# The first stage of a decoder trunk: weights loaded early into the room of later blocks, the conditioning row from TensorE, and each block's k-tiles ahead of its value parts

## The chip, the cores and the metric

One core of a Trainium2 chip runs the whole program. The metric is the device time of one execution in microseconds, the median of several runs. Before the change three runs took 2672.34, 2677.94 and 2679.41 us; the median is 2677.94.

## The reference, cut to what matters

The program is a two-layer decoder trunk for 256 positions of width 2048 in float32: a layer of RWKV-7 time mixing, a layer of latent attention, each followed by a squared-ReLU MLP. Ahead of every mixer stands a norm whose scale and shift come from a conditioning vector `c`:

```python
c_act = jax.nn.silu(c)
mod = (c_act @ ada_w[l] + ada_b[l]).reshape(B, N_MOD, 1, D)
h = rms_norm(x, norm_g[l, 0]) * (1.0 + scale_m) + shift_m
...
xx = token_shift(h) - h
xs = h[None] + xx[None] * mu[:, None, None, :]        # r, k, v, w, a, g
rkv = jnp.einsum('jbtd,jde->jbte', xs[:3], w_rkv)
w_log = -jax.nn.softplus(-(w0 + jnp.tanh(xw @ w1) @ w2)) - 0.5
a = jax.nn.sigmoid(a0 + (xa @ a1) @ a2)
g = jax.nn.sigmoid(xg @ g1) @ g2
```

The change touches the first stage alone: scale and shift of layer 0, the six shifted mixtures `xs`, the value projection, and the low-rank products behind `w`, `a` and `g`.

## The kernel before, in words

Products are made in split precision: a number is the sum of a high part, rounded to `fp32r`, and a low part, and a product is three matmuls (high x high, high x low, low x high). `hilo` (line 161) makes the parts: ACT casts, and another engine, DVE unless told otherwise, subtracts (line 163). Every weight comes through `load` (line 165): a tile `raw` of 128x2048, 1 MB, from the pool `wp`, which has three of them, and a DMA on SP's queue. That queue is in order: a load whose `raw` is still in use holds all behind it.

The first stage goes over the 16 k-tiles (128 input features each) in four blocks `cb` of four. For a block it needs

- scale and shift of its 512 features: `ada_pe` (line 271) for modulations 1 and 0, four loads `ada` each. PE multiplies them by the activated condition (line 278, `adap`), ACT copies, four matmuls sum (line 267, `modc`), DVE adds the bias (line 269, `mod`);
- small low-rank weights `lwa` and `lg1`, split once for the block;
- for each k-tile two transposes of the normed input (line 448, `trx`), `h` on ACT, the difference `d` to the position before, and six mixtures `xs` on DVE (line 457), each split by `hilo`. Mixtures 3, 4, 5 go into 12 low-rank matmuls `lr`, mixture 2 is kept for the block (`xsv`), mixtures 0 and 1 (r and k) are kept for the second stage in the four tiles `xsr`, `xsk` (high and low) of all 16 k-tiles.

`value_part(cb, n)` multiplies a block's `xsv` by one load `wv`: 24 matmuls `pv` (lines 202 to 204), whose result ACT copies or DVE adds to `V` (line 425). In the code the four value parts of block `cb - 1` stand ahead of the k-tiles of block `cb`, each with the next two steps of `ada_pe`:

```python
for n in range(4):
    next(at, 0)
    next(at, 0)
    if cb:
        value_part(cb - 1, n)
```

After block 3 its own value parts follow, and then the conditioning row `crow`, `silu(c)` repeated on 128 partitions: it is loaded as 1 MB, and ACT and DVE form exponential, sum, reciprocal and product in four pieces (lines 500 to 503). The remaining modulations are made from it on DVE during later stages (line 300, `ada_steps`). The second stage begins with `project_rk` (line 530): loads `wr` and `wk`, splits, and matmuls `rk`.

A scheduler turns this into one order for each engine; an engine runs its instructions strictly in that order. The pools set the waits: `p3` keeps three buffers of each k-tile tile (`h`, `d`, `xs`, `xlh`, `xll`), `split` two of each half weight.

## Time and profile before

| | |
|---|---|
| median of three runs | 2677.94 us |
| the profiled execution | 2670.03 us |
| its span | 2668.3 us |
| PE, DVE, ACT, POOL busy | 95%, 72%, 50%, 4% of the span |
| first stage | until about 221 us |
| DMA | 595.85 MB, 223 GB/s over the span |

The span is what the profiler saw of the engines in one execution; the execution's own time is 1.7 us longer. A row of a timeline gives the start from the span's beginning, how long it took, and, in brackets, how long the engine had been idle and which instruction ended that. A matmul's row includes its latency, so that rows of PE overlap.

### The profile page before, as it was taken

Reading aid. Unit: us, or ns where it says so; the run is one execution under the profiler, and the core shown is the slowest. Engines: PE = TensorE matmul, PEld = TensorE weight load, DVE = VectorE, ACT = ScalarE, POOL = GpSimd, SP = SyncE. Lnnn points to the kernel's source line nnn. Section 1 sums busy time; section 2 is a strip of 40 time slices with the busy share of each in tenths; the row PEclk is TensorE's granted clock in tenths of the full one; section 3 lists DMA queues with packets and bytes.
Section 4 is the critical chain, followed back from the end, with each engine's and each line's share of the span. In section 5 each row is a group of like instructions: output and inputs, shape, how many; then the busy total and the mean of one; then the engine's idle time right before and its main releaser. Section 6 shows DMA issues by size and latency. Waiting matters only on the chain.

```text
span 2668.3 us, 43143 instructions
## 1 busy us (share of the span) xinstructions
PE 2544.7 (95%) x16936; PEld 2191.4 (82%) x16936; DVE 1924.1 (72%) x3691; ACT 1327.1 (50%) x2361; POOL 105.2 (4%) x174
## 2 busy tenths in 40 slices
PE   6896899999998999999999998999899999999998
PEld 2576788888876899889988987788798998999896
DVE  4787788788877588888888757877667555555555
ACT  3543566666654544444444545554554444444443
POOL 0000111111100100000000002000010000000000
PEclk7998999999999999999999998999999999999999
DMA  8863444444456488888888831656657555555553
GB/s 314 302 235 144 171 167 155 158 167 159 148 207 269 172 333 329 332 334 324 339 321 329 327 141 72 237 188 241 233 183 270 185 187 191 186 188 189 189 190 127
DMA packets 88045, 595.85 MB, mean 223 GB/s; under 512 B 10144, under 2 KB 14496, under 8 KB 16800
## 3 DMA queue, kind: packets, MB, share of 16 engines
q1 hardware_dynamic: 87840, 593.08, 60.4%
q8 instruction: 133, 2.18, 0.3%
q14 instruction: 72, 0.59, 0.1%
HBM read 590.94 MB, written 2.10 MB: 222 GB/s over the span
## 4 chain that ended last, share of the span: by engine, by line
PE 87%; DVE 6%; ACT 3%; DMA 2%; issue 1%; POOL 1%; SPq 0%; DVEq 0%; ACTq 0%; POOLq 0%
PE pup L209 9%; PE pup L208 9%; PE pup L207 9%; PE pd L202 9%; PE pd L203 9%; PE pd L204 9%; PE rk L207 2%; PE rk L209 2%; PE rk L208 2%; PE pm L622 2%; DVE wlo L163 1%; PE po L203 1%; PE po L204 1%; PE po L202 1%; PE pv L203 1%
## 5 line engine op out<-in xcount | busy, mean ns | idle before, releaser
L163 DVE TENSOR_TENSOR wlo<-raw,whi 128x1024 fp32r<-128x1024 f32 (+1 forms) x737 | 877.3, 1193 | 478.2 <-ACT whi L162 475.4
L162 ACT CAST whi<-raw 128x1024 fp32r<-128x1024 f32 (+1 forms) x737 | 751.1, 1022 | 893.5 <-PE pd L204 380.6
L209 PE MATMUL pup<-hh,wlo 128*128 128x256 f32 x1920 | 543.5, 283 | 0.0
L207 PE MATMUL pup<-hh,whi 128*128 128x256 f32 x1920 | 543.4, 283 | 0.0
L208 PE MATMUL pup<-hl,whi 128*128 128x256 f32 x1920 | 543.3, 283 | 0.0
L202 PE MATMUL pd<-whi,uh 128*128 128x512 f32 x1024 | 398.7, 389 | 0.0
L203 PE MATMUL pd<-wlo,uh 128*128 128x512 f32 x1024 | 398.5, 389 | 0.0
L204 PE MATMUL pd<-whi,ul 128*128 128x512 f32 x1024 | 398.4, 389 | 0.0
L300 DVE SCALAR_TENSOR_TENSOR raw<-raw,crow 128x1024 f32<-128x1024 f32 x320 | 389.1, 1226 | 9.1 <-DMA raw<-in_adat_dram 9.0
L207 PEld LDWEIGHTS pup<-hh,whi 128*128 128x128 f32 x1920 | 368.6, 192 | 0.5
L208 PEld LDWEIGHTS pup<-hl,whi 128*128 128x128 f32 x1920 | 368.5, 192 | 0.5
L209 PEld LDWEIGHTS pup<-hh,wlo 128*128 128x128 f32 x1920 | 368.6, 192 | 0.0
L204 PEld LDWEIGHTS pd<-whi,ul 128*128 128x128 f32 x1024 | 192.2, 188 | 40.0
L202 PEld LDWEIGHTS pd<-whi,uh 128*128 128x128 f32 x1024 | 192.3, 188 | 39.5
L203 PEld LDWEIGHTS pd<-wlo,uh 128*128 128x128 f32 x1024 | 192.3, 188 | 39.3
L209 PE MATMUL rk<-xsrh,wlo 128*128 128x256 f32 x256 | 76.6, 299 | 15.7 <-DVE wlo L163 15.7
L207 PE MATMUL rk<-xskh,whi 128*128 128x256 f32 x256 | 81.2, 317 | 1.9 <-ACT whi L162 1.4
L207 PE MATMUL rk<-xsrh,whi 128*128 128x256 f32 x256 | 76.9, 301 | 3.0 <-ACT whi L162 3.0
L209 PE MATMUL rk<-xskh,wlo 128*128 128x256 f32 x256 | 75.1, 294 | 0.8 <-DVE wlo L163 0.8
L208 PE MATMUL rk<-xskl,whi 128*128 128x256 f32 x256 | 74.6, 291 | 0.0
L208 PE MATMUL rk<-xsrl,whi 128*128 128x256 f32 x256 | 74.5, 291 | 0.0
L209 PEld LDWEIGHTS rk<-xsrh,wlo 128*128 128x128 f32 x256 | 51.4, 201 | 16.8 <-DVE wlo L163 16.1
(433 smaller groups left out, 4094.1 us busy)
## 6 DMA issues: line engine op xcount, KB each, us to landing
raw<-in_adat_dram SPq DMA_DIRECT2D x160, 1024.0 KB, 6.8
raw<-in_up_dram SPq DMA_DIRECT2D x128, 1024.0 KB, 4.8
raw<-in_dn_dram SPq DMA_DIRECT2D x128, 1024.0 KB, 4.8
raw<-in_ada_dram SPq DMA_DIRECT2D x32, 1024.0 KB, 6.3
raw<-in_wv_dram SPq DMA_DIRECT2D x16, 1024.0 KB, 5.5
raw<-in_wr_dram SPq DMA_DIRECT2D x16, 1024.0 KB, 4.7
raw<-in_wk_dram SPq DMA_DIRECT2D x16, 1024.0 KB, 4.9
raw<-in_wo_dram SPq DMA_DIRECT2D x16, 1024.0 KB, 5.2
```

What stands on the lines that cost most here:

```text
L162: ACT.copy(hi, x)
L163: return eng.tensor_sub(lo, x, hi.bitcast(F32))
L202: PE.matmul(ps, lh, rh, start=start, stop=False)
L203: PE.matmul(ps, lh, rl, start=False, stop=False)
L204: PE.matmul(ps, ll, rh, start=False, stop=stop)
L207: PE.matmul(ps, wh, xh, start=start, stop=False)
L208: PE.matmul(ps, wh, xl, start=False, stop=False)
L209: PE.matmul(ps, wl, xh, start=False, stop=stop)
L300: DVE.scalar_tensor_tensor(raw[:, s], raw[:, s], 1.0, crow[:, s], ALU.mult, ALU.mult, accum_out=part[:, kt, half : half + 1])
L622: PE.matmul(pm[h][:, c * T : (c + 1) * T], lhs[hp, c * P : (c + 1) * P], AR[hp, c, :, :].rearrange("p x t -> p (x t)"), start=True, stop=True)
```

## The change

**Rooms.** The r and k mixtures lie no longer in four tiles of 16 k-tiles, but in one tile `xs{b}` per block b of 128x4x4x256, 16 KB per partition. Until block b writes its mixtures, its tile's room takes two weights of 1 MB: `load` asks `spot`, and after three loads into `raw` come two into each room that is still ahead (six before and in block 0 as the counter runs, then four, then two, none in block 3).

**Conditioning row.** `crow` is a tile for the whole program and is filled at the start: 16 matmuls spread the activated condition, column by column, over the partitions, and ACT copies four pieces. The load and DVE's twelve operations go.

**Order in a block.** The two `ada_pe` steps and the value part of the block before now follow each k-tile. The low parts of mixtures 0 and 1 are subtracted on POOL instead of DVE. The tiles of a k-tile lie in a pool of their own, `p6`, that ends with block 3; `zw`, `za` and `sg` are made after it and ahead of block 3's value parts.

```diff
     def load(src, n=2048, ahead=False):
+        raw = room_for[0]() if room_for[0] else None
+        if raw is not None:
+            SP.dma_start(raw[:, :n], src)
+            return raw
...
-        xsr_h = p1.tile([P, KT, T], F32R, tag="xsrh", name="xsrh")
...
+        XS = []
+        xs0 = p1.tile([P, 4, 4, T], F32R, tag="xs0", name="xs")
+        def xs_at(w, z, kt):
+            return XS[kt // 4][:, 2 * w + z, kt % 4, :]
...
+            def spot():
+                b_ = max(len(XS), 1)
+                at = spot_at[0] % (3 + 2 * (4 - b_))
+                spot_at[0] += 1
+                if at < 3:
+                    return None
+                if not spots:
+                    b_ += (at - 3) // 2
+                    t_ = p1.tile([P, 2, 2048], F32, tag=f"xs{b_}", name="early")
+                    spots.extend([t_[:, 0], t_[:, 1]])
+                return spots.pop(0)
+            room_for[0] = spot
...
+            for n in range(4):
+                ps = banks["pv"].tile([P, 512], F32, tag="pv", name="crows")
+                for j in range(4):
+                    kt = n * 4 + j
+                    PE.matmul(ps[:, j * P : (j + 1) * P], cact[:, kt : kt + 1].broadcast_to([P, P]), ident, start=True, stop=True)
+                ACT.copy(crow[:, n * 512 : (n + 1) * 512], ps)
...
-                for n in range(4):
-                    next(at, 0)
-                    next(at, 0)
-                    if cb:
-                        value_part(cb - 1, n)
-                for _ in at:
-                    pass
+                XS.append(p1.tile([P, 4, 4, T], F32R, tag=f"xs{cb}", name="xs") if cb else xs0)
+                spots.clear()
+                spot_at[0] = 0
...
-                        hilo(hi, lo, xs)
+                        hilo(hi, lo, xs, DVE if j >= 2 else POOL)
...
+                    next(at, 0)
+                    next(at, 0)
+                    if cb:
+                        value_part(cb - 1, kt - cb * 4)
+                for _ in at:
+                    pass
...
-            for n in range(4):
-                value_part(3, n)
+            room_for[0] = None
+            s1b.close()
+            pz = pool(sz, "pz", 1, side="right")
...
+            for n in range(4):
+                value_part(3, n)
...
-        raw = load(a["crow"], ahead=True)
-        for n in range(4):
-            s = slice(n * 512, (n + 1) * 512)
-            ACT.activation(crow[:, s], raw[:, s], AF.Exp, scale=-1.0)
-            DVE.tensor_scalar(crow[:, s], crow[:, s], 1.0, None, ALU.add)
-            DVE.reciprocal(crow[:, s], crow[:, s])
-            DVE.tensor_mul(crow[:, s], raw[:, s], crow[:, s])
```

How the order moves at three places (names are those of tiles, `L` a line of the kernel in question, and lines of the changed kernel differ from those of the profile):

The DMA queue on SP at the program's start, before (`L170` is `load`, `L393` the input `x`; a count is the number of equal rows):

```order
L170 DMA raw<-in_ada_dram 128x2048 x4
L393 DMA x<-in_x_dram 128x2048 x2
L170 DMA raw<-in_ada_dram 128x2048 x4
L170 DMA raw<-in_lwa_dram 128x768
L170 DMA raw<-in_lg_dram 128x1024
L170 DMA raw<-in_ada_dram 128x2048 x8
L170 DMA raw<-in_lwa_dram 128x768
L170 DMA raw<-in_lg_dram 128x1024
L170 DMA raw<-in_ada_dram 128x2048 x2
L170 DMA raw<-in_wv_dram 128x2048
```

and changed (`L176` is a load into `raw`, `L170` a load into a room, `early`):

```order
L176 DMA raw<-in_ada_dram 128x2048 x3
L170 DMA early<-in_ada_dram 128x2048
L423 DMA x<-in_x_dram 128x2048 x2
L170 DMA early<-in_ada_dram 128x2048 x4
L170 DMA early<-in_lwa_dram 128x768
L176 DMA raw<-in_lg_dram 128x1024
L176 DMA raw<-in_ada_dram 128x2048 x3
L170 DMA early<-in_ada_dram 128x2048 x5
L170 DMA early<-in_lwa_dram 128x768
L176 DMA raw<-in_lg_dram 128x1024
L176 DMA raw<-in_ada_dram 128x2048 x2
L176 DMA raw<-in_wv_dram 128x2048
```

Of the first eight `ada` five go to a room instead of to `raw`, and of the eight for block 1 five; the order of the inputs is the same.

DVE at the first stage's end, before (`L425` adds to `V`, `L501` to `L503` make the conditioning row, `L163` makes low parts, `L300` is a step of the later modulations):

```order
L501 TENSOR_SCALAR crow<-crow 128x512
L503 TENSOR_TENSOR crow<-raw,crow 128x512
L502 RECIPROCAL crow<-crow 128x512
L501 TENSOR_SCALAR crow<-crow 128x512
L503 TENSOR_TENSOR crow<-raw,crow 128x512
L502 RECIPROCAL crow<-crow 128x512
L501 TENSOR_SCALAR crow<-crow 128x512
L503 TENSOR_TENSOR crow<-raw,crow 128x512
L502 RECIPROCAL crow<-crow 128x512
L163 TENSOR_TENSOR wlo<-raw,whi 128x1024
L503 TENSOR_TENSOR crow<-raw,crow 128x512
L300 SCALAR_TENSOR_TENSOR raw,adpart<-raw,crow 128x1024 x2
```

and changed (`L455` adds to `V`, `L306` is the step):

```order
L455 TENSOR_TENSOR V<-pv_1880,V 128x512
L455 TENSOR_TENSOR V<-pv_1881,V 128x512
L163 TENSOR_TENSOR wlo<-raw,whi 128x1024
L306 SCALAR_TENSOR_TENSOR raw,adpart<-raw,crow 128x1024 x2
L163 TENSOR_TENSOR wlo<-raw,whi 128x1024
L455 TENSOR_TENSOR V<-pv_1918,V 128x512
L455 TENSOR_TENSOR V<-pv_1919,V 128x512
L163 TENSOR_TENSOR wlo<-raw,whi 128x1024
L306 SCALAR_TENSOR_TENSOR raw,adpart<-raw,crow 128x1024
L163 TENSOR_TENSOR wlo<-raw,whi 128x1024
L306 SCALAR_TENSOR_TENSOR raw,adpart<-raw,crow 128x1024
L163 TENSOR_TENSOR wlo<-raw,whi 128x1024
```

The twelve operations of the conditioning row are gone, and the low parts of the first `wr` weights stand right behind and between the last additions to `V`.

POOL in blocks 0 to 3, before (`L450` clears a column of `h`, `L527` clears the `Tt` tiles of the second stage):

```order
L347 MEMSET ssx 128x2
L450 MEMSET h 128x1 x13
L527 MEMSET Tt_1986 128x512
L527 MEMSET Tt_1988 128x512
L527 MEMSET Tt_1990 128x512
L574 MEMSET cum 128x2
```

and changed, in block 3 (`L476` clears a column of `h`):

```order
L476 MEMSET h 128x1
L163 TENSOR_TENSOR xs<-xs 128x256
L476 MEMSET h 128x1
L163 TENSOR_TENSOR xs<-xs 128x256 x2
L558 MEMSET Tt_1987 128x512
L558 MEMSET Tt_1989 128x512
L558 MEMSET Tt_1991 128x512
L163 TENSOR_TENSOR xs<-xs 128x256 x6
L605 MEMSET cum 128x2
```

POOL had only small clearings here; now two subtractions per k-tile stand among them, 32 in all, the last six behind the clearing of `Tt`.

## Rows read from the trace of the kernel before

**Rows 1.** The head of the page.

```profile
span 2668.3 us, 43143 instructions
```

**Rows 2.** The table by stretch: the stretch and its length in us, then for each engine its busy time in us and its instructions, TensorE's granted clock, the mean share of the 16 DMA engines, GB/s.

```profile
0.00:40.50 40.50, 20.19 (x84) 6.17 (x84) 6.82 (x26) 8.23 (x15) 1.60 (x18) 0.77 0.81 307
40.50:86.00 45.50, 37.32 (x212) 21.48 (x216) 39.85 (x99) 25.93 (x56) 0.70 (x7) 0.83 0.90 333
86.00:133.00 47.00, 42.26 (x232) 28.40 (x232) 34.00 (x81) 27.38 (x51) 0.40 (x4) 0.96 0.77 286
170.00:201.00 31.00, 30.97 (x149) 24.91 (x148) 30.01 (x59) 16.10 (x28) 1.75 (x6) 1.00 0.49 170
222.00:239.00 17.00, 2.09 (x17) 1.89 (x17) 17.00 (x12) 0.40 (x3) 0.00 (x0) 0.63 0.00 0
6.00:26.00 20.00, 9.34 (x41) 2.75 (x41) 3.29 (x14) 5.19 (x9) 0.10 (x1) 0.80 0.99 403
```

**Rows 3.** The waits of the DMA queue on SP in the first 245 us: who waited, for whom, us in total, times, longest.

```profile
SPq L170 <- PE adap L278: 72.3, 32, 4.9
SPq L170 <- DVE wlo L163: 53.5, 9, 20.8
```

**Rows 4.** The timeline of DVE: the additions that complete the second of the two modulations (shift, `mods[0, 0]`) of blocks 0 to 3. Columns: start us, us, engine, line, operation, tiles, [idle time before it <- what ended it].

```profile
40.28 0.16 DVE L269 TENSOR_TENSOR mod<-modc,pcol 128x4 f32<-128x4 f32 x1 [11.79 <-PE modc L267]
...
66.94 0.16 DVE L269 TENSOR_TENSOR mod<-modc,pcol 128x4 f32<-128x4 f32 x1 [3.85 <-PE modc L267]
...
109.58 0.16 DVE L269 TENSOR_TENSOR mod<-modc,pcol 128x4 f32<-128x4 f32 x1 [7.97 <-PE modc L267]
...
156.93 0.16 DVE L269 TENSOR_TENSOR mod<-modc,pcol 128x4 f32<-128x4 f32 x1 [2.92 <-PE modc L267]
```

**Rows 5.** The tile `crow` (the conditioning row): count, then ns min/median/max, first and last start in us, form.

```profile
L502 DVE RECIPROCAL crow<-crow x4: 3344/3346/3353, 221.9 to 234.3; 128x512 f32<-128x512 f32 x4
L503 DVE TENSOR_TENSOR crow<-raw,crow x4: 677/678/678, 225.4 to 238.7; 128x512 f32<-128x512 f32 x4
```

**Rows 6.** The timeline of PE around the end of the first stage, columns as in rows 4.

```profile
223.49 0.28 PE L207 MATMUL rk<-xsrh,whi 128*128 128x256 f32 x1
223.61 0.28 PE L208 MATMUL rk<-xsrl,whi 128*128 128x256 f32 x1
238.79 0.58 PE L209 MATMUL rk<-xsrh,wlo 128*128 128x256 f32 x1 [14.91 <-DVE wlo L163]
239.17 0.41 PE L207 MATMUL rk<-xsrh,whi 128*128 128x256 f32 x1
239.39 0.41 PE L208 MATMUL rk<-xsrl,whi 128*128 128x256 f32 x1
```

**Rows 7.** The timeline of DVE in blocks 0 and 2: runs of equal operations that follow one another without idle time between them, so that (us of the run less one operation's 0.48, 0.42, 1.22 or 0.69) over (count less one) is the distance.

```profile
47.55 1.27 DVE L457 SCALAR_TENSOR_TENSOR xs<-d,pcol,h 128x256 f32<-128x256 f32 x3
...
53.90 1.09 DVE L163 TENSOR_TENSOR xll<-xs,xlh 128x256 fp32r<-128x256 f32 x3
...
145.81 2.36 DVE L163 TENSOR_TENSOR wlo<-raw,whi 128x1024 fp32r<-128x1024 f32 x2 [0.84 <-ACT whi L162]
...
152.62 1.39 DVE L425 TENSOR_TENSOR V<-pv,V 128x512 f32<-128x512 f32 x2 [4.45 <-PE pv L204]
```

**Rows 8.** The tile `hl`, a low part that POOL makes in a later stage: count, ns min/median/max, first and last start, form.

```profile
L163 POOL TENSOR_TENSOR hl<-hc,hh x16: 1267/1290/2245, 875.5 to 1948.1; 128x512 fp32r<-128x512 f32 x16
```

**Rows 9.** The timeline of POOL there.

```profile
894.44 2.02 POOL L163 TENSOR_TENSOR hl<-hc,hh 128x512 fp32r<-128x512 f32 x1 [0.22 <-ACT hh L162]
```

**Rows 10.** The timeline of DVE at the same time.

```profile
893.88 4.80 DVE L163 TENSOR_TENSOR wlo<-raw,whi 128x1024 fp32r<-128x1024 f32 x3 [0.49 <-ACT whi L162]
```

**Rows 11.** The timeline of PE in block 1 (transposes, value matmuls, `ada` matmuls, low-rank matmuls, column sums; each matmul is shown with its latency, the distance of two starts is what it takes of PE) and the last value matmul of the stage.

```profile
77.17 0.44 PE L448 MATMUL trx<-ident,x 128*128 128x128 f32 x2
...
79.03 0.73 PE L202 MATMUL pv<-whi,xsv 128*128 128x512 f32 x2
...
81.14 0.40 PE L203 MATMUL pv<-wlo,xsv 128*128 128x512 f32 x1
81.38 0.40 PE L204 MATMUL pv<-whi,xsv 128*128 128x512 f32 x1
...
85.91 1.92 PE L278 MATMUL adap<-raw,c 128*32 128x512 f32 x16
...
88.07 0.28 PE L209 MATMUL lr<-xlh,lwa 128*96 128x256 f32 x1
88.19 0.28 PE L207 MATMUL lr<-xlh,lwa 128*96 128x256 f32 x1
...
89.49 0.95 PE L267 MATMUL modc<-sel,adap 128*128 128x1 f32 x8
...
220.39 0.40 PE L204 MATMUL pv<-whi,xsv 128*128 128x512 f32 x1
```

**Rows 12.** DMA issues in the first 260 us: count, KB each, median us to landing.

```profile
raw<-in_ada_dram SPq DMA_DIRECT2D x32, 1024.0 KB, 6.3
raw<-in_wv_dram SPq DMA_DIRECT2D x16, 1024.0 KB, 5.5
raw<-in_lg_dram SPq DMA_DIRECT2D x4, 512.0 KB, 4.3
raw<-in_lwa_dram SPq DMA_DIRECT2D x4, 384.0 KB, 3.0
```

More of the change, by code (lines that the diff above doesn't have):

```diff
@@ L336, in scale_cols @@
         return t
+    crow = pool(ctx, "crow", 1).tile([P, D], F32, name="crow")
     ap_ = pool(ctx, "ap", 1)
@@ L365, in trunk_kernel @@
     with ExitStack() as s0:
-        sps = s0.enter_context(ExitStack())
+        sps, sz = (s0.enter_context(ExitStack()) for _ in range(2))
         psum(sps, pv=4, lr=2, rw=1, ad=1)
@@ L485, in trunk_kernel @@
             for g in range(2):
-                gt = p3.tile([P, T], F32, tag="xs", name="gt")
+                gt = p3.tile([P, T], F32, tag="gt", name="gt")
                 ACT.activation(gt, pg[g], AF.Tanh, scale=0.5)
@@ L533, in project_rk @@
                 res = []
-                for w, (xh, xl) in enumerate(((xsr_h, xsr_l), (xsk_h, xsk_l))):
-                    raw = load(a["wr" if w == 0 else "wk"][i])
+                for w, name in enumerate(("wr", "wk")):
+                    raw = load(a[name][i])
                     o = slice(w * T, (w + 1) * T)
@@ L904, in trunk_kernel @@
             junk_p[0] = pool(ctx, "junk", 1, side="right")
[L905 removed]
+            G0 = p1.tile([P, KT, T], F32R, tag="xs3", name="G0").bitcast(F32).rearrange("p k c -> p (k c)")
             split["more"] = pool(s3, "more", 3)
```

50 lines of the change are left out of this document (24 added, 26 removed).

## The prediction

> **What bounds the kernel now.** I read four views in this order. The table by stretch says which engine is full where: up to 40.5 us PE is busy half of the time and the DMA engines have a share of 0.81, up to 86 us 0.90, then 0.77; from 170 to 201 us PE is busy 30.97 of 31 us; from 222 to 239 us PE does 2.09 us of work, DVE 17.00 of 17, and DMA moves nothing [rows 2]. So the head of the first stage waits for transfers, its end is held by PE, and behind it stands a hole that belongs to DVE alone. The span is 2668.3 us [rows 1], so all that the change touches lies in the first tenth. The DMA queue's own waits say why the head is slow: SP sits 72.3 us behind PE's reading of `adap` weights and 53.5 us behind DVE's `wlo` [rows 3]. Both are waits for one of the three `raw` buffers. The `mod` rows on DVE are the stage's milestones: block 0's modulation is ready at 40.28 us, block 1's at 66.94, block 2's at 109.58, block 3's at 156.93 [rows 4]. The hole is the conditioning row: four reciprocals of 3.35 us and four products of 0.68 on DVE [rows 5], while the second half of the first `wr` split stands behind them and PE idles 14.91 us [rows 6].
>
> **The hole goes.** 4 x (3.346 + 0.678) = 16.1 us of DVE, with the four short additions 17.5, leave the queue; the `wlo` behind them follows the last `V` addition at once. PE gets back its 14.91 us. The first matmuls behind the hole start 0.21 us apart, those before it 0.12 [rows 6]: the clock was at its lower level after the idle time. Some 21 of them cost (0.21 - 0.12) x 21 = 2.0 us more. Sum: -16.9 us. What replaces it, 16 matmuls of 128x128 and four ACT copies behind the first `adap` group, is unpriced in this trace for its operands; the nearest rows are two transposes of the same shape in 0.44 us [rows 11], so 16 cost about 3.5 us and twice that at the lower clock. They lie where PE is busy 20.19 of 40.5 us waiting for weights [rows 2]; cover gone, they would cost at most 7 us, otherwise 0. I take 0. One load of 1 MB falls out of the queue at a place where DMA moves nothing: 0.
>
> **The early weights.** Before block 0, 10 loads of 1 MB (8 `ada`, 2 `x`; sizes in [rows 12]) and half a MB of tables go out: 11.0 MB. Now PE's progress on three buffers paces the eight `ada`; after the change three of them take those buffers and five go into rooms that nobody has to free first. In the stretch where nothing holds the queue it moved 403 GB/s at a share of 0.99 [rows 2]. A share of 0.99 for 0.81 over 40.5 us would save 7.4 us; the PE, ACT and DVE steps behind the last load stay, so I take 6: block 0's modulation at 34 us. The Trainium skill speaks against such a rate: the page "DMA: Bandwidth & Descriptors", section "Where 436 GB/s comes from", says that for transfers from HBM the HBM side, about 358 GB/s, binds. The trace does not agree in this stretch (403), and the measurement decides; by the page the 11.0 MB would take 3.4 us longer, and the forecast would be that much later.
>
> Further back I use 370 GB/s, which is 333 at a share of 0.90 brought to 1 [rows 2]. Block 1 needs 8 `ada`, `lwa`, `lg`: 9.3 MB, 25 us, modulation at 59 us (now 66.94). The queue then brings two `ada` and the first `wv`; with the 0.9 MB ahead of them 4.05 MB or 11 us, plus a split of ACT and DVE, and the first `pv` matmul starts at 68 us instead of 79.03 [rows 11]. Up to block 2's last `ada` it is 12.4 MB or 33.6 us more (modulation near 92), up to block 3's 13.5 MB or 36.5 us (near 129); then transfers stop being the limit.
>
> **What PE still has to do from there.** 384 `pv` at 0.233 us apart: 89.5; 16 `ada` loads of 8 rows at 0.116: 14.8; 120 `lr` matmuls at 0.12: 14.4; four `modc` groups at 0.95: 3.8; 20 transposes at 0.22: 4.4; together 126.9 us [rows 11]. Now it takes from 79.03 to 220.6, 141.6 us: 14.7 lost. After the change the end of the stage lies between 68 + 126.9 = 195 (nothing lost) and 68 + 141.6 = 209.6 (as much lost as now).
>
> **The low parts on POOL** decide where between. 32 subtractions of 128x256 leave DVE, 0.34 us each as they follow one another [rows 7]: -10.7 us. POOL's 128x512 subtraction takes 1.29 us [rows 8], so half of it, 0.64, here; upper bound the whole 1.29. But they are not free for DVE: while one of them stood on POOL from 894.44 us [rows 9], three `wlo` took 4.80 us [rows 10] where 3 x 1.14 + 0.08 = 3.50 is usual [rows 7]. DVE lost 1.30 us, the whole POOL operation. The Trainium skill has this as a rule that speaks against the change: "SBUF — State Buffer", section "Who interferes with whom", says that a DVE instruction with two SBUF inputs and a GpSimd one that reads SBUF exclude each other for the whole instruction. The trace agrees; without the exclusion DVE would gain 10.7 us and I would forecast the 195 end, with it DVE loses about 10.
>
> There is a wait besides. The three `xs` buffers now come free through POOL for two of six products, and the next k-tile's second and third product on DVE wait for that; behind them in DVE's queue stand its `xll`, `xsv` and the `wlo` of the value weights, for which PE waits. A k-tile costs DVE now 0.34 + 6 x 0.40 + 6 x 0.34 = 4.8 us [rows 7]; after it 4.1 plus the stretch from the last product over two ACT casts (0.82) and two POOL operations (1.29, with 0.2 of handing over), of which 0.74 is covered by the difference and one product: 5.7. With 8 halves of `wlo` at 1.14, 8 additions to `V` at 0.70 [rows 7] and 2 us for `lwa` and `lg`, a block takes DVE 2 + 22.8 + 9.1 + 5.6 = 39.5 us, as much as PE's 22.4 + 7.4 + 5.8 + 1.9 + 1.8 = 39.3. Two level engines that feed each other don't run without loss: I take half of what is lost now, 7 us, and the end at 202 us. Block 0's chain, 2 + 4 x 5.7 = 25 us from 34, ends at 59, level with block 1's modulation, so it costs nothing there.
>
> **Moved and free:** the value part of the block before now follows each k-tile instead of all standing ahead of the block. No DMA and no matmul is added, and the order from `wr` on is as before on SP, so I leave the rest of the program at 0; a shift of some 3 us either way is in the range. `zw`, `za`, `sg` wait for the buffers of the k-tiles and are needed only by the second stage.
>
> **Sum** against the profiled execution, 2670.03 us: the stage's end 220.6 -> 202, -18.6; the hole -16.9; together -35.5, 2634.5 us. The median of the runs shown, 2677.94, is 7.9 above that execution; from it the forecast is **2642.4 us**, I write 2642.
>
> **Rivals.** *Only the hole goes:* the DMA engines had a share of 0.90 up to 86 us already, and PE is full from 170 on [rows 2]; with POOL in DVE's way the earlier arrivals are eaten up and the stage ends at 220 as now. Then -16.9: 2661. It decides if block 2's modulation is not ready well before 109 us. *More than forecast:* the 195 end, because DVE's lock rarely falls on a path: -25.6 - 16.9 = -42.5, 2635, and to 2627 if the first `pv` starts by 60. *Slower, by one mechanism:* a room is the buffer of block b's own split rows, so b's first ACT cast into it waits until the weights in it are used up, among them a `wv` of block b-1; ACT and SP are in order, and if that wait holds back the rest, chain and transfers of a block stop overlapping. Then blocks 1 and 2 take 25 + 34 us (12.6 MB at 370), block 3 25 + 22.4, the last values 22.4: 59 + 118 + 47.4 + 22.4 = 246.8 against 220.6 + 16.9 = 237.5 that the hole makes of it now: +9.3, 2687. It decides from 12 us of such waiting per block on ((237.5 - 202) / 3). Against it: what lies in room 1 is mostly `ada`, which block 1 must have used anyway, and the queue keeps 9, 7, then 5 loads ahead. *It doesn't do what it says:* `raw` keeps only three places and every second load goes there, so that the room loads stand behind a `raw` load that waits; then the head stays as it is, and this is the first rival again.
>
> **Chances.** A measurement of this kernel tells about 0.3%, 8 us, from no change. Forecast (2630 to 2653) 0.66; only the hole 0.18; more 0.08: these are faster by over 0.3%, 0.92. Slower 0.04; the remaining 0.04 is a mix of gain and new waits that cancel. The range goes from 2627 (more than forecast, with its earliest start) to 2662 (only the hole); the bounds of POOL's price, 0 and 1.29 us an operation, move the stage's end between 195 and some 215 and lie inside.
>
> **What would show it.** Right: `mod` rows near 34, 59, 92 and 129 us; DMA share over 0.9 up to 120 us; the first `pv` near 68 and the last near 202; 32 POOL subtractions of 0.6 to 1.3 us with DVE products beside them stretched; `rk` matmuls that follow the last `pv` with no idle time over 3 us. Wrong: `mod` of block 2 still near 105 (transfers or POOL held the chain); an ACT cast into `xs` that waits over 5 us for a DMA or PE (the slower rival); a hole at the stage's end with another name; a second stage that takes over 5 us longer than before.

## The result

The changed kernel takes **2649.86 us**, the median of four runs (2648.88 to 2655.09); the kernel before took 2678.68 (four runs, 2672.34 to 2679.46). The ratio is 0.9902, with a 95% interval of 0.9881 to 0.9922. The profiled execution takes 2650.15 us, its span is 2648.4, against 2670.03 and 2668.3 before [rows 1]. The medians are 28.8 us apart, the profiled executions 19.9, since before's profiled execution lies 8.7 us below its median and after's does not. The accounts below are between profiles unless a median is named.

The forecast was 2642 us within 2627 to 2662. The time lies in the range, but the forecast expected half of the gain from the first stage and half from the hole behind it, and the trace shows nearly all of it in the hole.

### The profile page after: what moved, and what is told of

The parts are those of the page before. It is cut to its first block, busy times and chain, and to the rows that moved or that the text cites. A ratio compares the mean times of both kernels' runs of the same rounds, so it can differ in the third digit from the quotient of the medians.

```text
span 2648.4 us, 43182 instructions
## 1 busy us (share of the span) xinstructions
PE 2545.9 (96%) x16968; PEld 2191.6 (83%) x16968; DVE 1903.9 (72%) x3647; ACT 1326.1 (50%) x2361; POOL 135.3 (5%) x206
## 4 chain that ended last, share of the span: by engine, by line
PE 88%; DVE 6%; ACT 3%; issue 1%; DMA 1%; POOL 0%; SPq 0%; DVEq 0%; ACTq 0%; POOLq 0%
PE pup L215 9%; PE pup L214 9%; PE pup L213 9%; PE pd L208 9%; PE pd L210 9%; PE pd L209 9%; PE rk L213 2%; PE rk L215 2%; PE rk L214 2%; PE pm L653 2%; DVE wlo L163 1%; PE adap L284 1%; PE pv L209 1%; PE pv L210 1%; PE pv L208 1%
## 5 line engine op out<-in xcount | busy, mean ns | idle before, releaser
L163 DVE TENSOR_TENSOR wlo<-raw,whi 128x1024 fp32r<-128x1024 f32 (+1 forms) x731 | 871.3, 1195 | 478.6 <-ACT whi L162 476.4
L306 DVE SCALAR_TENSOR_TENSOR raw<-raw,crow 128x1024 f32<-128x1024 f32 x320 | 387.6, 1221 | 11.6 <-DMA raw<-in_adat_dram 11.5
L213 PE MATMUL rk<-xs,whi 128*128 128x256 f32 x512 | 156.9, 306 | 2.8 <-ACT rS L580 2.2
L215 PE MATMUL rk<-xs,wlo 128*128 128x256 f32 x512 | 151.3, 295 | 2.2 <-DVE wlo L163 2.2
L214 PE MATMUL rk<-xs,whi 128*128 128x256 f32 x512 | 148.4, 290 | 0.0
L213 PEld LDWEIGHTS rk<-xs,whi 128*128 128x128 f32 x512 | 100.1, 195 | 14.2 <-issue 9.3
L215 PEld LDWEIGHTS rk<-xs,wlo 128*128 128x128 f32 x512 | 99.9, 195 | 4.9 <-DVE wlo L163 3.0
L214 PEld LDWEIGHTS rk<-xs,whi 128*128 128x128 f32 x512 | 100.0, 195 | 0.9
L717 DVE TENSOR_TENSOR xt<-ar,X 128x60 f32<-128x60 f32 (+14 forms) x240 | 49.5, 206 | 20.2 <-ACT ar L706 17.5
## 6 DMA issues: line engine op xcount, KB each, us to landing
early<-in_ada_dram SPq DMA_DIRECT2D x17, 1024.0 KB, 11.6
```

The costliest lines, as they stand in the source:

```text
L163: return eng.tensor_sub(lo, x, hi.bitcast(F32))
L213: PE.matmul(ps, wh, xh, start=start, stop=False)
L214: PE.matmul(ps, wh, xl, start=False, stop=False)
L215: PE.matmul(ps, wl, xh, start=False, stop=stop)
L306: DVE.scalar_tensor_tensor(raw[:, s], raw[:, s], 1.0, crow[:, s], ALU.mult, ALU.mult, accum_out=part[:, kt, half : half + 1])
L717: DVE.tensor_tensor(xt[:, :, :n], ar[:, :, o : o + n], X[:, :, j : j + 1].broadcast_to([P, 4, n]), ALU.mult)
```

## The profile after

The end of the first stage comes first. The timeline of PE (start us, us, engine, line, operation, tiles, [idle time before it <- what ended it]):

```profile
219.50 0.40 PE L210 MATMUL pv<-whi,xsv 128*128 128x512 f32 x1
219.74 0.28 PE L213 MATMUL rk<-xs,whi 128*128 128x256 f32 x1
219.85 0.28 PE L214 MATMUL rk<-xs,whi 128*128 128x256 f32 x1
220.13 0.39 PE L215 MATMUL rk<-xs,wlo 128*128 128x256 f32 x1
...
227.19 0.39 PE L213 MATMUL rk<-xs,whi 128*128 128x256 f32 x1 [1.29 <-ACT rS L580]
```

The hole is gone: behind the last `pv` the `rk` matmuls follow without idle time, 0.12 us apart, and up to 242 us the longest idle time is 1.29 us. Before there were 14.91 us, and then 0.21 us from start to start [rows 6]. But the stage itself ends at 219.74 us, where before it ended at 220.63.

The first `po` matmul, a landmark at the second stage's end, stood at 834.15 us before and stands at 815.27 now. So the account in spans is: first stage 220.63 to 219.74, **-0.9**; from there to `po` 613.5 to 595.5, **-18.0**; the rest 1834.1 to 1833.1, -1.0; together -19.9 us.

The timeline of DVE, the milestones of [rows 4]:

```profile
35.58 0.16 DVE L275 TENSOR_TENSOR mod<-modc,pcol 128x4 f32<-128x4 f32 x1 [7.36 <-PE modc L273]
...
63.33 0.16 DVE L275 TENSOR_TENSOR mod<-modc,pcol 128x4 f32<-128x4 f32 x1 [4.12 <-PE modc L273]
...
107.08 0.16 DVE L275 TENSOR_TENSOR mod<-modc,pcol 128x4 f32<-128x4 f32 x1 [8.73 <-PE modc L273]
...
153.89 0.16 DVE L275 TENSOR_TENSOR mod<-modc,pcol 128x4 f32<-128x4 f32 x1 [2.92 <-PE modc L273]
```

Blocks 0 to 3 get their modulation 4.7, 3.6, 2.5 and 3.0 us earlier than before. The lead of the head is not built up further, it is lost on the way: the forecast had 6, 8, 18 and 28.

The table by stretch, columns as in [rows 2] (stretch, length, busy us and instructions of PE, weight loads, DVE, ACT, POOL; granted clock, DMA share, GB/s):

```profile
0.00:40.50 40.50, 23.85 (x126) 11.17 (x127) 11.48 (x35) 14.39 (x26) 1.60 (x18) 0.83 0.89 350
40.50:86.00 45.50, 39.73 (x216) 19.81 (x214) 38.05 (x81) 23.34 (x53) 13.17 (x21) 0.89 0.90 370
86.00:133.00 47.00, 43.08 (x234) 28.93 (x231) 28.95 (x55) 24.66 (x45) 5.08 (x9) 0.96 0.69 260
133.00:170.00 37.00, 34.45 (x180) 25.28 (x180) 27.57 (x48) 16.96 (x32) 9.27 (x10) 0.95 0.65 233
170.00:201.00 31.00, 29.09 (x135) 23.56 (x134) 30.17 (x67) 17.43 (x34) 8.23 (x13) 0.94 0.36 128
```

The DMA share has risen to 0.89 in the head, and from 86 to 133 us it has fallen from 0.77 to 0.69. From 86 to 170 no engine is full: PE 77.5 of 84 us, DVE 56.5. From 170 to 201 DVE is.

The waits of the DMA queue on SP in the first 245 us (for whom, us in total, times, longest), to be held against [rows 3]:

```profile
SPq L176 <- DVE wlo L163: 61.3, 13, 9.1
SPq L176 <- PE adap L284: 31.9, 10, 6.6
SPq L170 <- PE adap L284: 23.7, 4, 7.2
SPq L176 <- DVE xll L163: 23.3, 4, 7.9
SPq L176 <- DMA raw<-in_lg_dram: 20.7, 2, 12.5
```

The queue still stands: L176 is a load into one of the three `raw`, L170 a load into a room. The wait for `adap` has fallen from 72.3 to 55.6 us (31.9 and 23.7), that for `wlo` has risen from 53.5 to 61.3 on the loads into `raw` alone. Standing behind `xll` and behind landings is not new: 30.4 and 22.9 us before.

How this looks in the queue's order (timeline of SP, columns as above):

```profile
19.31 19.66 SPq L176 DMA_DIRECT2D raw<-in_ada_dram  x3
39.05 2.64 SPq L170 DMA_DIRECT2D early<-in_ada_dram  x5
...
47.41 3.14 SPq L176 DMA_DIRECT2D raw<-in_ada_dram  x2
66.39 0.33 SPq L176 DMA_DIRECT2D raw<-in_wv_dram  x1
...
86.49 0.33 SPq L170 DMA_DIRECT2D early<-in_ada_dram  x1
```

Five loads into rooms that are free stand behind three `raw` loads that take from 19.31 to 38.97 us to issue. The first `wv` waits for a `raw` until 66.39, 16 us after the load ahead of it, and everything behind waits with it.

A queue that stands costs the stage time only where an engine then waits for a load. From 19.3 to 39.0 us the DMA engines had a share of 0.93 all the same, with the loads issued before. And from 45 us to the end of the stage no wait of PE, its weight loads, ACT or DVE ends with the landing of a load. Before, these did (45 to 220 us):

```profile
ACT whi L162 <- DMA raw<-in_wv_dram: 2.7, 2, 2.2
...
ACT lg L162 <- DMA raw<-in_lg_dram: 1.1, 2, 0.7
...
PEld adap L278 <- DMA raw<-in_ada_dram: 0.8, 1, 0.8
```

From issue and time to landing one can tell when each load was there. Block 2's last `ada` (what the issue took in ns, when it stood in us, and the time to landing), before:

```profile
L170 SPq DMA_DIRECT2D raw<-in_ada_dram x1: 327/327/327, 97.8 to 97.8; - x1
...
DMA to landing us min/median/max: 6.7/6.7/6.7
```

and after:

```profile
L170 SPq DMA_DIRECT2D early<-in_ada_dram x1: 328/328/328, 86.5 to 86.5; - x1
...
DMA to landing us min/median/max: 5.9/5.9/5.9
```

It landed at 104.5 us before and lands at 92.4 now, 12.1 us earlier, but block 2's modulation is ready only 2.5 us earlier. The same reckoning for the loads from block 1 on: each `ada` had landed 3 to 15 us before PE took it, and the stand of the queue ahead of the first `wv` made no engine wait either: it landed at 71.1 us and ACT cast it at 76.0.

What holds the modulation shows ahead of block 2. DVE:

```profile
95.99 2.36 DVE L163 TENSOR_TENSOR wlo<-raw,whi 128x1024 fp32r<-128x1024 f32 x2 [3.14 <-ACT whi L162]
107.08 0.16 DVE L275 TENSOR_TENSOR mod<-modc,pcol 128x4 f32<-128x4 f32 x1 [8.73 <-PE modc L273]
107.16 2.36 DVE L163 TENSOR_TENSOR wlo<-early,whi 128x1024 fp32r<-128x1024 f32 x2
```

and PE at the same time:

```profile
97.67 0.62 PE L208 MATMUL pv<-whi,xsv 128*128 128x512 f32 x2
...
103.03 0.40 PE L210 MATMUL pv<-whi,xsv 128*128 128x512 f32 x1
103.36 1.06 PE L284 MATMUL adap<-raw,c 128*32 128x512 f32 x8
104.24 1.04 PE L284 MATMUL adap<-early,c 128*32 128x512 f32 x8
105.98 1.05 PE L273 MATMUL modc<-sel,adap 128*128 128x1 f32 x8 [0.70 <-ACT adap L288]
```

DVE has done its k-tiles of block 1 and idles 8.73 us. PE is busy, but with a value part of block 0; the last two `ada` steps of block 2 stand behind it in PE's order, though the last weight they need has lain there since 92.4 us, and only then can DVE begin the next block. In all (waits of DVE from 30 to 222 us), before:

```profile
DVE mod L269 <- PE modc L267: 29.6, 7, 11.8
...
```

and after:

```profile
DVE mod L275 <- PE modc L273: 24.4, 6, 8.7
DVE wlo L163 <- ACT whi L162: 8.1, 8, 3.1
DVE V L455 <- PE pv L210: 6.6, 3, 4.5
DVE xll L163 <- ACT xlh L162: 4.3, 3, 1.7
DVE d L479 <- ACT h L477: 2.9, 1, 2.9
DVE xs L482 <- POOL xs L163: 0.6, 1, 0.6
```

Of the wait for the modulation 11.8 us before and 7.4 after are block 0's. Behind block 0 it was 17.8 us and is 17.0: the change hardly touched it.

The low parts on POOL, groups by line up to 222 us (busy us, mean ns | idle time before), after:

```profile
L482 DVE SCALAR_TENSOR_TENSOR xs<-d,pcol,h 128x256 f32<-128x256 f32 x96 | 49.5, 561 | 0.9 <-POOL xs L163 0.6
L163 POOL TENSOR_TENSOR xs<-xs 128x256 fp32r<-128x256 f32 x32 | 33.0, 1044 | 53.5 <-ACT xs L162 53.2 <-ACT h L477 0.3
```

and the products before:

```profile
L457 DVE SCALAR_TENSOR_TENSOR xs<-d,pcol,h 128x256 f32<-128x256 f32 x96 | 41.9, 479 | 0.2
```

## The experiments

Theory 1: the gain is the hole, and the first stage did not move because the three `raw` buffers and the one queue still pace the modulations, so that DVE waits for them. Rivals: POOL's low parts eat up what the rooms bring; the new order of a block does; the stage is bound by PE, or by DVE, and no earlier weight can help it. One more follows from the landings above, and no experiment was planned for it: the weights are there in time, and the modulations come late because of where their matmuls stand in PE's order.

"Stage end" is the first `rk` matmul (before 220.6, after 219.7), "wait" what DVE waits for `modc` behind block 0's modulation, up to 222 us, "mods" the milestones of blocks 0 to 3. Each ratio is to runs of the kernel before that were made beside it, whose median was 2671.8 to 2678.7.

| run | median us | ratio [95%] | mods | stage end | wait |
|---|---|---|---|---|---|
| before | | | 40.3 66.9 109.6 156.9 | 220.6 | 17.8 |
| after | 2649.86 | 0.9902 [0.9881, 0.9922] | 35.6 63.3 107.1 153.9 | 219.7 | 17.0 |
| e1_hole | 2653.36 | 0.9926 [0.9907, 0.9944] | 41.4 68.1 110.9 159.8 | 225.7 | 17.9 |
| e2_dve_lo | 2648.99 | 0.9907 [0.9887, 0.9927] | 36.6 65.6 108.3 157.5 | 222.4 | 17.6 |
| e3_lg_room | 2650.46 | 0.9914 [0.9894, 0.9935] | 35.9 63.8 107.5 157.9 | 221.4 | 16.9 |
| e4_ada_first | 2652.02 | 0.9925 [0.9905, 0.9945] | 36.2 64.4 99.6 145.5 | 221.4 | 17.8 |
| f1_two_products | 2639.07 | 0.9862 [0.9842, 0.9882] | 36.3 64.1 104.3 148.9 | 211.8 | 14.1 |
| f2_no_rooms | 2661.08 | 0.9938 [0.9918, 0.9958] | 40.0 69.8 115.4 164.6 | 231.0 | 19.1 |
| f3_one_ada | 2618.19 | 0.9788 [0.9759, 0.9816] | 27.5 53.5 90.6 130.1 | 193.7 | 1.9 |
| f4_no_vadd | 2646.57 | 0.9881 [0.9860, 0.9903] | 36.6 64.5 108.3 155.1 | 217.0 | 22.8 |
| g1_old_order | 2658.57 | 0.9943 [0.9923, 0.9962] | 36.7 67.0 110.8 159.2 | 236.8 | 24.3 |
| g2_old_dve | 2644.71 | 0.9897 [0.9877, 0.9918] | 36.5 63.0 104.1 149.5 | 219.1 | 21.2 |
| g3_old_dve_lg | 2646.72 | 0.9908 [0.9886, 0.9930] | 34.8 62.9 105.5 150.8 | 220.4 | 22.8 |
| h1_half_ada | 2637.11 | 0.9866 [0.9849, 0.9882] | 33.1 62.8 102.2 142.9 | 206.7 | 2.9 |

Two cautions: the scheduler makes a new order of every kernel, so an edit moves more than itself; and spans of single profiles are not compared here below 10 us (why is told at the end), stage ends are.

**e1_hole**: the kernel before with the conditioning row from PE, at the end of the first stage.

```diff
+        crow = pool(ctx, "crow", 1, side="right").tile([P, D], F32, name="crow")
+        for n in range(4):
+            ps = banks["pv"].tile([P, 512], F32, tag="pv", name="crows")
...
+                PE.matmul(ps[:, j * P : (j + 1) * P], cact[:, kt : kt + 1].broadcast_to([P, P]), ident, start=True, stop=True)
+            ACT.copy(crow[:, n * 512 : (n + 1) * 512], ps)
         sps.close()
-        raw = load(a["crow"], ahead=True)
...
```

> The kernel before, with one part of the change alone: the conditioning row comes from 16 matmuls and four ACT copies where its load and its twelve DVE operations stood, at the end of the first stage. Theory (nearly all of the gain is the hole): PE's 14.9 us of idle time at 224 us go, the 2 us at the lower clock too, and some 3.5 us of matmuls come in their place, so 13 to 14 us less than before; the last value matmul stays at 220.6 us. Rival (the hole is worth less, since transfers that it hid become a wait of their own): under 8 us less, and a new wait for wr or wk right behind it. The changed kernel should then be only 3 to 6 us below this one, the matmuls among them.

It gets 19 us of the change's 28.8 by medians; its interval and that of the change overlap. The stage end of 225.7 has 3.5 us of the 16 matmuls in it, since here they stand at the stage's end; the last `pv` is at 221.9.

**e2_dve_lo**: the changed kernel with the low parts of mixtures 0 and 1 on DVE.

```diff
-                        hilo(hi, lo, xs, DVE if j >= 2 else POOL)
+                        hilo(hi, lo, xs)
```

> The changed kernel with the low parts of mixtures 0 and 1 on DVE again. Theory (POOL and DVE exclude each other, so the move costs DVE more than it saves): the mean of an xs product goes back from 561 to 480 ns, the waits of xs for POOL go, the last value matmul comes 3 to 8 us earlier than 219 us. Rival (POOL relieves DVE on balance): it comes 3 to 8 us later, since 32 subtractions of 0.34 us stand on DVE again.

The products are back at 476 ns, the stage ends 2.7 us later, the time is the same. In this order POOL neither helps nor harms by more than that.

**e3_lg_room**: the low-rank weights `lwa` and `lg1` lie in the room of block 3 instead of in `raw`.

```diff
+                lwr = p1.tile([P, 2, 2048], F32, tag="xs3", name="lwr")
-                    raw = load(a[z][cb], n)
+                    raw = lwr[:, e_]
+                    SP.dma_start(raw[:, :n], a[z][cb])
...
-                at = spot_at[0] % (3 + 2 * (4 - b_))
+                at = spot_at[0] % (3 + 2 * (3 - min(b_, 3)))
```

> The changed kernel with the two low-rank weights of a block in the room of block 3 instead of in raw (ada and wv use raw and the rooms of blocks 1 and 2). Theory (lg sits in one of three raw buffers until its block begins, and SP, in order, stands behind it from 20 to 39 and from 50.6 to 66.4 us, the room loads too): these two stands go, the DMA share up to 86 us rises over 0.95, the first value matmul starts at 68 to 71 instead of 77.1 us, and the last ends 4 to 8 us earlier than 219. Rival (the blocks are paced by PE, DVE and POOL, 44 to 47 us each, and earlier weights only wait): the first value matmul comes earlier, but the last ends within 2 us of 219.

The queue's wait for `lg` is gone, and its wait for `adap` is 83.2 us (78.0 and 5.2) instead of 55.6: the stand moves to the next `raw` load. The stage ends 1.6 us later.

**e4_ada_first**: four modulation steps after each of the first two k-tiles, none after the others.

```diff
-                    next(at, 0)
-                    next(at, 0)
+                    for _ in range(4 if kt - cb * 4 < 2 else 0):
+                        next(at, 0)
```

> The changed kernel with four steps of ada_pe behind each of a block's first two k-tiles instead of two behind each of four. Theory (the next block's modulation is late because its last ada columns stand on PE behind the third value part, not for lack of weights): modulation of block 2 at 92 to 98 instead of 107 us, of block 3 at 138 to 145 instead of 154, and the last value matmul 4 to 8 us earlier than 219. Rival (PE has the same work in another order and is full): the modulations come earlier and the end stays within 2 us of 219. Second rival (the queue): the eight loads are not there yet, and PE waits for ada in block 1.

Blocks 2 and 3 have their modulation 7.5 and 8.4 us earlier, but the first `pv` stands at 87.2 instead of 77.1 us. Its weight landed at 77.1 us (issued at 68.3, 8.8 us to landing) and ACT cast it at 85.7, so it did not wait for the queue. DVE's wait stays at 17.8 us and the stage ends 1.7 us later: in the order of the engines, what is brought forward pushes the other back.

**f1_two_products**: the value parts lose one of three products (high part of the weight by low part of the mixture), 128 `pv` matmuls or 29.8 us of PE.

```diff
-                down_units([a["wv"][n, cb]], *xsv[cb], pss, list(range(4)))
...
+                            PE.matmul(pss[t], xsv[cb][0][:, at_, q], hi[:, s], start=at_ == 0, stop=False)
+                            PE.matmul(pss[t], xsv[cb][0][:, at_, q], lo[:, s], start=False, stop=at_ == 3)
```

> The changed kernel whose value parts leave out the product with the low part of the mixture: 256 value matmuls instead of 384. All else stands, the loads, splits and additions too. Theory (PE holds the first stage: from block 0's modulation to the end it is occupied some 168 of 184 us, whatever the order): 128 x 0.233 = 29.8 us less work, and the last value matmul comes 22 to 30 us earlier than 219 us. Rival (the chain of DVE, POOL and ACT paces the blocks, PE's time is stretched by waiting for it): it comes under 12 us earlier. Rival (transfers): under 8 us earlier, with more waits for DMA.

Of 29.8 us 8.0 arrive at the stage's end. From block 0's modulation to the end PE is busy 19.9 us less (147.8 for 167.7), with a granted clock of 0.89 in the stretch where the change has 0.94, and its idle time grows by 11.4 us. So PE's work alone does not bound the stage, though PE is busy over nine tenths of it.

**f2_no_rooms**: all loads go to `raw`.

```diff
-            room_for[0] = spot
+            room_for[0] = None
```

> The changed kernel with every load into raw, none into a room. Theory (PE holds the stage; rooms only move the head): block 0's modulation at about 40 us again instead of 35.6, the first value matmul some 2 us later, the last at 220 to 224 us. Rival (the rooms keep PE fed through the whole stage and their gain is eaten by POOL or the order): the last value matmul at 228 us or later.

The stage ends 11.3 us later than with rooms, and 10.4 later than before. So within this order the rooms are worth 11 us, 4.4 of them ahead of block 0's modulation. And here the engines do wait for landings from 45 us on, ACT 5.9 us, PE and its weight loads 5.7, where the change has no such wait. The two longest sums:

```profile
ACT whi L162 <- DMA raw<-in_wv_dram: 4.5, 2, 4.2
...
PEld adap L284 <- DMA raw<-in_ada_dram: 3.9, 3, 2.3
```

That is what the rooms take away.

**f3_one_ada**: of the four loads of a group one is made, and PE multiplies it four times; 24 loads, 25.2 MB, are left out.

```diff
-            raw = load(a["ada"][m, cb, g], ahead=True)
+            if g == 0:
+                raw = load(a["ada"][m, cb, g], ahead=True)
```

> The changed kernel that loads one of four ada pieces of a modulation and uses it four times: 24 MB of transfers less in the first stage, with the same PE work. Theory (PE holds the stage): block 0's modulation near 25 us instead of 35.6, no stand of SP for ada, and the last value matmul earlier by the head's gain at most, 6 to 11 us; the stretch from block 0's modulation to the end stays 180 to 187 us. Rival (transfers and the three raw buffers still pace the blocks): that stretch shrinks by over 10 us.

The only edit that moves the stage as far as the forecast thought it would move, and further: it ends at 193.7 us with PE's work unchanged, and the waits of DVE from 30 to 222 us now read

```profile
DVE wlo L163 <- ACT whi L162: 15.5, 14, 3.1
...
DVE mod L275 <- PE modc L273: 1.9, 1, 1.9
...
```

Behind block 0, 17.0 us of waiting for the modulation have become 1.9. Of the 26.0 us 8.1 are an earlier block 0, the other 17.9 come between block 0's modulation and the end. Not all of that is waiting: the same matmuls keep PE busy 160.2 us there instead of 167.7, at a granted clock of 0.98 instead of 0.94, and its idle time is some 10 us shorter.

**f4_no_vadd**: DVE's additions to `V` for blocks 1 and 2 are left out, 11 us.

```diff
-                    else:
+                    elif cb == 3:
```

> The changed kernel without the 16 additions of the value parts of blocks 1 and 2 to V: 11 us of DVE's time less, spread over blocks 2 and 3. Theory (PE holds the stage): the last value matmul stays within 2 us of 219. Rival (DVE, stretched by POOL, paces blocks 2 and 3): it comes 5 to 11 us earlier.

2.8 us arrive; DVE's wait for the modulation grows from 17.0 to 22.8. Of the work taken from DVE in the middle of the stage, about half becomes waiting.

**g1_old_order**, **g2_old_dve**, **g3_old_dve_lg**: the old order of a block with the rooms and the early row; g1 with the low parts on POOL, g2 on DVE, g3 as g2 with e3's edit.

```diff
+                for n in range(4):
+                    next(at, 0)
+                    next(at, 0)
+                    if cb:
+                        value_part(cb - 1, n)
+                for _ in at:
+                    pass
                 ks = slice(cb * 4, cb * 4 + 4)
...
-                    next(at, 0)
-                    next(at, 0)
-                    if cb:
-                        value_part(cb - 1, kt - cb * 4)
-                for _ in at:
-                    pass
```

> The changed kernel with the rooms, the early conditioning row and the low parts on POOL, but with the order of a block as before: the steps for the next block's modulation and the value parts of the block before stand ahead of the k-tiles. It does the whole computation. Without the rooms the changed kernel ended its first stage 11 us later (231.0 instead of 219.7 us), 10 us later than the kernel before (220.6). Theory A: that loss of 10 us is the price of the new order; with the old one the rooms bring their 11 us in full, and the first rk matmul starts at 208 to 212 us and the time falls to about 2640 (ratio 0.987). Theory B: the loss is POOL's exclusion of DVE, then this kernel ends its stage at 218 to 222 like the changed one. Theory C: the three raw buffers and the queue pace any order, then 218 to 222 too, and the next kernel of this call shows the same.

> As the run before it in this call, and the low parts of mixtures 0 and 1 on DVE again: the kernel before with the rooms and the early conditioning row alone. Theory A (order costs): stage end 208 to 214 us, ratio about 0.987. Theory B (POOL costs): stage end 8 to 10 us earlier than in the run before it, which stands at 218 to 222. Theory C (the queue paces whatever the order): both at 218 to 222, ratio 0.990 to 0.992.

> As the run before it, and the low-rank weights lwa and lg1 lie in the room of block 3, so that no raw buffer is held by them until the k-tiles' split; only the rooms of blocks 1 and 2 are left for ada and wv. Theory A and B: the queue's stand of some 8 to 12 us on lg goes, block 0's modulation stays at 36 us, block 1's falls by 2 to 5 us and the stage's end by 2 to 5 against the run before it. Theory C: as in the changed kernel, where the same edit left the end at 221.4 instead of 219.7 us, the wait only moves: the end within 3 us of the run before it.

Theory A fell: g1 ends at 236.8, 17 us later than the change, and not at 208 to 212. For g2 and g3 theory C's 218 to 222 holds, and g1 lies outside all three. Of theory B the size is exceeded: with the low parts on POOL the old order ends its stage 17.7 us later and takes 13.9 us more by medians, where in the new order the move costs nothing. The milestones of g1 fall behind g2's block by block (+0.2, +4.0, +6.7, +9.7). About half of the 17.7 us shows as a lower clock of TensorE: from block 0's modulation on the same matmuls keep PE busy 173.9 us in g1 and 164.6 in g2, at a granted clock of 0.90 and 0.95. Whether POOL's waits bring the clock down is open. DVE waits 3.5 us for POOL directly; through which waits the rest goes is not settled, since the two kernels' last `wv` loads also issue 8 us apart. g2 and the change end their stage together and take the same time: so the new order and the POOL move, made together, bring nothing that the old order with DVE did not have, nor do they cost anything. No version that does the whole work beats the change by more than the interval. g3 repeats e3: 1.3 us later.

The table by stretch of g2 from 6 to 86 us is remarkable:

```profile
6.00:86.00 80.00, 61.24 (x348) 32.49 (x348) 41.40 (x108) 34.56 (x67) 0.60 (x6) 0.85 1.00 411
```

Here DMA never pauses for 80 us, at 411 GB/s, and still the stage ends at 219.1 us with a wait of 21.2 us for the modulation behind block 0: from 86 to 133 us its share is 0.62 and the queue waits for `raw` again. From 45 us on no engine waits for a landing here either. Transfers that run ahead at the head do not by themselves shorten the stage.

**h1_half_ada**: every early `ada` load brings half its columns, 16.8 MB less, and PE multiplies that half twice; the loads have almost the same order and the same buffers.

```diff
-            raw = load(a["ada"][m, cb, g], ahead=True)
+            raw = load(a["ada"][m, cb, g][:, :1024], 1024, ahead=True)
...
-                PE.matmul(ps[32 * j : 32 * j + 32, :], c32[:, kt, :], raw[:, j * 512 : (j + 1) * 512],
+                PE.matmul(ps[32 * j : 32 * j + 32, :], c32[:, kt, :], raw[:, j % 2 * 512 : (j % 2 + 1) * 512],
```

> The changed kernel whose 32 early ada loads bring half of their columns (0.5 MB instead of 1), while PE multiplies as many columns as before (the half it has, twice): it leaves out half of that weight. Number, order and buffers of the loads are nearly as in the changed kernel; 16.8 MB of traffic are gone. The kernel with one ada load of four (24 of 32 loads and 25.2 MB gone) ended its stage 25 us earlier, at 194.8 us, but it took away both the bytes and most of the waits for a raw buffer. Theory A (bytes: the DMA engines' rate paces the stage): two thirds of that, stage end near 203 us, block 2's modulation near 96, DMA share of the first 86 us still about 0.9. Theory B (holds: the queue stands behind raw buffers that PE and DVE have to free, and bytes count only until the first of them): block 0's modulation at 29 to 32 us, but block 2's above 100, the stage's end at 212 to 219, and a DMA share well under 0.8 in the first 86 us.

(The expectation has f3's end as 194.8 us; its first `rk` matmul stands at 193.7.) The result lies between the two theories: the stage ends at 206.7 us (A said 203), block 2's modulation is at 102.2 (B: above 100), and the DMA engines are far from full (B):

```profile
0.00:40.50 40.50, 26.50 (x131) 10.42 (x131) 11.03 (x33) 12.73 (x23) 1.60 (x18) 0.84 0.71 255
40.50:86.00 45.50, 42.94 (x241) 23.09 (x240) 39.13 (x85) 26.70 (x59) 14.29 (x21) 0.99 0.65 239
```

So fewer bytes shorten the stage without the DMA engines being the limit. Through what is not shown. An `ada` load into `raw` lands after 5.9 us instead of 8.6 (medians), one into a room after 7.5 instead of 11.6, but in the change too the loads behind block 0 lay ready before PE took them. DVE's wait for the modulation falls from 17.0 to 2.9 us, and 10.6 of the 13.1 us lie behind block 0's modulation. PE's order is another one here: it starts on the first four `ada` of block 2 between 63.0 and 66.1 us, in the change between 68.1 and 85.4, though two had landed by 64.5 and all four by 76.1.

What the runs show together: the stage's end follows neither PE's work alone (f1) nor DVE's (f4) nor a fuller DMA head (g2). It moves far only where DVE's wait for the modulations goes (17.0 and 219.7, 2.9 and 206.7, 1.9 and 193.7); that half of theory 1 stands. The other half, that the queue and the three `raw` buffers cause this wait, does not follow: behind block 0 the change's engines wait for no load. The queue's stand does cost time where loads come too late for an engine, as in f2. What f3 and h1 gain behind block 0 may come from another order on PE, from the higher clock, or from both; no run changes one of these alone. e4 changed the order in the code, and its wait stayed.

## Why the prediction was right, and which step of it failed

**The hole: right.** -16.9 forecast, -18.0 measured between `rk` and `po`; with the edit alone the same stretch is 16.7 us shorter (613.5 to 596.8) and the median falls by 19 (e1). The 16 matmuls were set to cost nothing in the head; the change's block 0 is 4.7 us earlier in spite of them, and no run prices them alone.

**The head: nearly right.** Block 0's modulation was forecast at 34 us, it came at 35.6. The Trainium skill's page "DMA: Bandwidth & Descriptors", section "Where 436 GB/s comes from", lets the HBM side bind at about 358 GB/s. The measurement decided otherwise again, more clearly than in the trace of before: 411 GB/s over 80 us in g2.

**The step that failed** is the one from transfers to modulations, which ends "then transfers stop being the limit". It let the modulations follow one another at the pace of the loads, bytes over 370 GB/s: 59, 92, 129 us, each at the same distance behind its last `ada`. For blocks 1 and 2 the loads nearly kept that pace: the last `ada` of blocks 0 to 2 landed at 31.7, 56.6 and 92.4 us. Only block 3's came late, at 143.9; from 86 to 133 us the queue moved 260 GB/s. But the modulations were ready 4 us behind the landing in block 0 and 7, 15 and 10 us behind it in blocks 1 to 3, at 63.3, 107.1 and 153.9 us. What the way from a landed weight to the modulation gains in length, through an order on PE in which the `ada` steps stand behind k-tiles and value parts, was put at nothing. The prediction had a sign of it in its own sums: a block costs DVE 39.5 us and PE 39.3, more than the 33 and 37 at which it let blocks 2 and 3 follow. In f3, with 24 loads gone, they follow in 37.1 and 39.5, in the change in 43.8 and 46.8. The first rival, "only the hole", came true for the stage, with 0.18; its criterion, that block 2's modulation is not ready well before 109 us, was met: 107.1. Of the last rival the stand is real, but not its effect: the head did not stay as it was, and the loads did come earlier.

**From the first `pv` to the end.** The end was forecast at 202 and came at 219.7, by two terms. The first `pv` came at 77.1 instead of 68: its weight landed at 71.1, and ACT cast it only at 76.0. The way from there was put at 126.9 us of PE's work and 7 lost, half of what was lost before; it took 142.6, so 15.7 were lost, before 14.7. "Two level engines that feed each other" was the right picture, but DVE's waiting for modulations had not gone. Nor was the sum's clock the real one: its prices are those at full clock, and the granted clock of the stretch was 0.94. Even f3 loses 9.9 (136.8 from 56.9).

**POOL: right in kind.** A subtraction was put at 0.64 us and bound by 1.29: the fastest takes 0.73, the mean is 1.04. That DVE pays was forecast: the products' mean went from 479 to 561 ns, 32 operations' worth of relief (10.7 us) less 7.6 us of stretching. The Trainium skill ("SBUF — State Buffer", "Who interferes with whom") has this exclusion, and the trace agrees: in e2, with no POOL subtraction beside them, the products are at 476 ns. What POOL does to the stage's end depends on the order: nothing over 3 us here; in g1 against g2 17.7, with the clock's part in it.

**The slower rival** did not come: the 32 casts into `xs` have 8.5 us of idle time before them, all of it for DVE's products, none for a DMA or PE. The rooms bring 11 us in this order (f2), 3.1 in the old one (the last `pv` of e1 against g2's, 221.9 and 218.8).

**Why the time lies in the range all the same.** Of the signs that were named, the row of `rk` behind the last `pv`, the POOL operations and a second stage that is not longer came as forecast; the later two milestones and a DMA share over 0.9 up to 120 us did not. By profiles the gain is 19.9 us, and the first rival's price for it was 16.9. By medians it is 28.8, because the profiled execution of before was 8.7 us faster than its median and the one of after was not. So the time lies in the range because the hole alone reaches it; that it came nearer to 2642 than the rival's 2661 is luck of the executions, and not a gain of the first stage.

## What to carry to other kernels

More room for early weights takes away the waits of the engines for landings; that it brings anything beyond them no run here shows. Before such a change, compare when each load lands with when an engine first takes it, and add up the waits that end with a landing: from 45 us on these were under 5 us in the kernel before, where the forecast promised 18.6 for the whole stage, 6 of them for the head. The waits of the DMA queue and its bytes do not tell this; behind block 0 the queue stood for tens of us while every load came in time. Where weights lie ready and the next step still comes late, look at what stands ahead of it in the order of the engine that takes them. Whether an order exists that brings this stage forward, or whether loads with a free place should be issued first, no run here shows. An operation alone on the path with everything else idle, as the conditioning row was, is the cheapest gain to find: it stands in the table by stretch as one engine at its full length and the others at nothing.

## What was not expected of the hardware

The granted clock falls in different places in kernels whose code is the same there. From 640 to 740 us, in the second stage, the changed kernel has

```profile
640.00:740.00 100.00, 97.47 (x853) 77.63 (x851) 80.17 (x269) 63.82 (x178) 12.39 (x20) 0.91 0.41 148
```

and e2_dve_lo

```profile
640.00:740.00 100.00, 96.78 (x888) 79.13 (x887) 85.70 (x288) 66.10 (x181) 13.64 (x20) 1.00 0.45 165
```

PE was busy 97 of 100 us in both, yet the mean clock is 0.91 in one, a mixture of the two levels, and 853 matmuls are shown instead of 888. From 660 to 680 us it is 0.71, and there the longest idle time of PE is 0.46 us. The second stage from `rk` to `po` took 595.5 us in the one, with PE busy 571.9, and 585.2 in the other, with PE busy 560.5; 586.6 in g2, 588.7 in g3. What brings the clock down there no run shows; about 10 us of a single profile's span hang on it, which is why this study reads stage ends.

And the 32 POOL subtractions of the changed kernel, of one shape (count, ns min/median/max, first and last start):

```profile
L163 POOL TENSOR_TENSOR xs<-xs x32: 730/898/3328, 42.1 to 190.0; 128x256 fp32r<-128x256 f32 x32
```

One operation takes from 0.73 to 3.33 us. Its price taken as half of a 128x512 one (0.64) lay below the fastest.
